# Residual state kept in HBM during the up projection, its memory used for early weight blocks of the down projection

## The chip, the cores and the metric

The kernel runs on one core of one Trainium2 chip, in one launch. The metric is device microseconds of the run. In the profile PE is TensorE's matmuls and PEld its weight loads, DVE is VectorE, ACT ScalarE, POOL GpSimd and SP SyncE, which issues most of the transfers.

## The reference

One layer of a decoder for 256 tokens of width 2048, all in float32. Shortened:

```python
def layer(x, p, mix_norm_g, w_in, ..., w_out, ffn_norm_g, w_up, conv_w, conv_b, w_down, ple_norm_g, w_ple_gate, w_ple_proj):
    h = rms_norm(x, mix_norm_g)
    z = h @ w_in                                   # one projection for both groups of mixers
    a = mlstm(z)                                   # 4 matrix-memory heads, chunkwise
    b = forgetting_attention(z)                    # 8 causal heads with log-forget bias
    x = x + concat([a, b]) @ w_out
    u = rms_norm(x, ffn_norm_g) @ w_up             # (256, 2 * 5632)
    u = gelu(causal_dwconv(u[:, :5632], conv_w, conv_b)) * u[:, 5632:]
    x = x + u @ w_down
    return x + sigmoid(rms_norm(x, ple_norm_g) @ w_ple_gate) * (p @ w_ple_proj)
```

The inner width is 5632, which is 44 blocks of 128 ("K tiles") of the down projection.

## The kernel before

**Products in float32.** Each weight block of 128 x 1024 values (512 KB) is loaded from HBM into a raw buffer by SP, cast by ScalarE to a high part `hi` (L969, L282 in the first stages), and VectorE makes the low part `lo = raw - hi` (L970, L284). PE then does three matmuls for each product, hi x hi, hi x lo and lo x hi, into a PSUM bank of 128 x 512. The step that needs one block is a *unit*. A unit of the up projection or of a plain pair has 12 matmuls. There are three raw buffers, and four buffers for parts; from the down projection on, two more buffers for parts exist (`w2`, made free by an earlier tile), two more raw buffers (`w2raw`), and later further rooms for raw blocks: `pT`, the two halves of `EZ` and part of `Y` (`ring`). `free_raws` says which rooms a block may use, and the loop in `run_units` loads a block as soon as a room is free and splits units up to six ahead of the unit that PE works on.

**The residual state.** `xs` holds x, 256 tokens by 2048 columns, as two tiles of 128 tokens: 2 MB of SBUF. The output projection's column groups add their results to `xs` (`resid`, L785), 512 columns at a time, square-sum them and send them to be transposed (squares on VectorE, then moves into `x2z` issued by POOL, then columns scaled into `x2T`). During the up projection nothing reads or writes `xs`. It is read again by `sums_done` (L1117 to L1122) and `add_rest` (L1130) at the end of each half of the down projection.

**Up projection.** Eleven groups of 16 units each. After a group, ScalarE scales the result into `EZ` (L869), VectorE transposes 32 x 32 squares (L193), POOL issues moves back into `EZ` (L199), and `up_act` does the convolution (L886 on ScalarE, eight L889 on VectorE), the GELU (L895), the gate product (L896) and the split into high and low parts (L138 for `uC`). For the last group these jobs are hung behind units of the down projection, at the positions (5, 6, 6, 7, 8, LAST_UP) with LAST_UP = 9.

**Down projection.** It has two halves of 1024 columns, and each goes through 22 pairs of K tiles. A plain pair is two units with four products each. The nine pairs in `SEVEN` use seven block products in place of eight (a Strassen-like scheme) and are four units with 1, 2, 2 and 2 products: for them VectorE also makes four differences of the raw blocks (L1065, L1066, L1075, L1076), and sums of the left operand are computed in the up projection, stored in HBM by POOL (L855) and loaded again by SP. The products that more than one result needs (P1, P5, P6, P7) gather in banks of their own (`dnP`), and `sums_done` adds them to `xs` behind the last of the sevens. `FIRST` gives the order of the pairs in the first half; the second half goes in the order 0 to 21. In the first half the last four pairs on the list are 19, 18, 20 and 21.

**What sets the order.** The program is written in units, but the build lets a scheduler order the instructions of each engine within the dependencies, so an instruction can stand at another place in its engine's queue than in the code. Each engine then runs its queue in order. SP's queue of loads is also in order: a load that waits holds the loads behind it.

Of the kernel before, what the change touches and what calls it, by code (L numbers as in the profile page):

```python
# [9 lines left out]
F32 = mybir.dt.float32  # L10
# [5 lines left out]
P = 128  # L16
S = 256
NT = S // P
D = 2048
# [5 lines left out]
KF = FF // P  # L25
# [7 lines left out]
BLK = 1024  # L33
# [1 line left out]
PARTS2 = 2  # L35

SEVEN = (2, 4, 6, 8, 10, 12, 14, 16, 18)
FIRST = (0, 1, 3, 5, 2, 7, 4, 6, 9, 8, 11, 10, 13, 12, 15, 14, 17, 16, 19, 18, 20, 21)
AHEAD_DMA, AHEAD_SPLIT = 3, 3
PAD = 16  # L40


LO_SHIFT = 16
FRONT = 12
LAST_UP = 9


@with_exitstack
def layer_kernel(
# [6 lines left out]
    nc = tc.nc  # L56
    act, dve, pe, pool = nc.scalar, nc.vector, nc.tensor, nc.gpsimd
# [7 lines left out]
    mp = mixers.enter_context(tc.tile_pool(name="mix", bufs=1))  # L65
    kp = ctx.enter_context(tc.tile_pool(name="kept", bufs=1, space=bass.MemoryType.DRAM))
    ps = ctx.enter_context(tc.tile_pool(name="ps", bufs=4, space=bass.MemoryType.PSUM))

    def bank(tag, name):
        return ps.tile([P, 512], F32, tag=tag, name=name)  # L70
# [11 lines left out]
    xs = bp.tile([P, NT, D], F32, name="xs")  # L82
# [61 lines left out]
    def transpose_x(dst, k0, g, tag="aux"):  # L144

        for k in (k0, k0 + 1):
            bk = bank(tag, f"xT{k}")
            for t in range(NT):
                pe.transpose(bk[:, t * P : (t + 1) * P], xs[:, t, k * P : (k + 1) * P], ident)
            split_T(dst[:, k, :], bk[:, 0:256], scale=g[:, k : k + 1])  # L150

    def sumsq(ssq, c, n):
        for t in range(NT):
            junk = sm.tile([P, 512], F32, tag="junk", name="junk")[:, :n]
            act.activation(junk, xs[:, t, c * n : (c + 1) * n], AF.Square, accum_out=ssq[:, t, c : c + 1])
# [29 lines left out]
    def squares(name):  # L185

        return mp.tile([P, NT, 4, 128], F32, tag="sq", name=name)

    def square(y, t, k, src):

        n = src.shape[1] // P
        o = y[:, t, :, 32 * k : 32 * (k + n)].rearrange("p b (k j) -> p k b j", j=32)
        dve.transpose(o, src)  # L193
# [7 lines left out]
    def gather(y, name):  # L201
        c = mp.tile([P, NT * 4, 128], F32, tag="col", name=name)
        move(y, c)
        return c, done[0]
# [8 lines left out]
    def columns(yz, dst, k0, gain):  # L213

        c, start = yz
        while not since(7, start):
            yield
        for k in range(4):
            column(c, k, dst()[:, k0 + k], gain[:, k0 + k : k0 + k + 1])
            yield  # L220
# [159 lines left out]
    with mixers:  # L380
# [399 lines left out]
        def resid(c, ssq, dst, gain):  # L780
            st = {}

            def f(t, b):
                xc = xs[:, t, c * 512 : (c + 1) * 512]
                dve.tensor_add(xc, b, xc)  # L785
                if c < 3:
                    if t == 0:
                        st["y"] = squares("x2y")
                    square(st["y"], t, 0, xc)
                if t == NT - 1:  # L790
                    if c < 3:
                        side.append(columns(gather(st["y"], "x2z"), dst, c * 4, gain))
                    else:
                        for k0 in (c * 4, c * 4 + 2):
                            transpose_x(dst(), k0, gain)
                    sumsq(ssq, c, 512)
            return f

        kcat = all_k[4:] + all_k[:4]
# [17 lines left out]
    with tc.tile_pool(name="ffn", bufs=1) as fp:  # L817
        x2 = x2T["t"]
# [15 lines left out]
        ring = Y[:, 0:1536].rearrange("p (r c) -> p r c", r=3)  # L834
# [5 lines left out]


        sums = kp.tile([len(SEVEN), P, 1024], F32, name="sums")

        def left_sums(p_, u):

            (a11, a21), (a12, a22) = ((u[:, j, 0:P], u[:, j, P:S]) for j in range(2))
            f = sm.tile([P, 512], F32, tag="junk", name="Sf").rearrange("p (i c) -> p i c", i=4)
            dve.tensor_add(f[:, 0], a21, a22)
            dve.tensor_sub(f[:, 1], f[:, 0], a11)
            dve.tensor_sub(f[:, 2], a11, a21)  # L850
            dve.tensor_sub(f[:, 3], a12, f[:, 1])
            t = fp.tile([P, 4, 256], F32R, tag="pT", name="Sp")
            act.copy(t[:, :, 0:P], f)
            dve.tensor_sub(t[:, :, P:256], f, f32(t[:, :, 0:P]))
            pool.dma_start(out=sums[SEVEN.index(p_)], in_=f32(t).rearrange("p i c -> p (i c)"))  # L855
# [48 lines left out]
        late = {}  # L904
        made, now = [0], [0]
        room = {"raw": RAW}
        taken, used = deque(), {}

        def free_raws(j):

            def may(t):
                return (t not in ("pT", "ring") or j < late["gate"]) and (t not in ("e0", "e1", "ring") or now[0] > late["free"])

            return sorted((t for t in room if taken.count(t) < room[t] and may(t)), key=lambda t: used.get(t, -1))

        def new_raw(j, name):
            tag = free_raws(j)[0]
            taken.append(tag)
            used[tag] = len(used) and max(used.values()) + 1
            if tag == "ring":  # L920
                return ring[:, 0:2].rearrange("p a b -> p (a b)")
            if tag in ("e0", "e1"):
                return EZ[:, int(tag[1])]
            if tag == "raw":
                return wp.tile([P, BLK], F32, tag="raw", name=name, bufs=RAW)
            if tag == "late":
                if tag not in late:
                    late[tag] = apool.tile([P, 2, BLK], F32, tag="aTb", name="w2raw", bufs=2)
                    late["n"] = 0
                late["n"] += 1  # L930
                return late[tag][:, late["n"] % 2]
            return fp.tile([P, BLK], F32, tag=tag, name=name, bufs=room[tag])
# [42 lines left out]
        def run_units(us, first_late, gate):  # L975
            loaded = split = 0
            for i, u in enumerate(us):
                if i == first_late:
                    v = apool.tile([P, 6, BLK], F32R, tag="aTa", name="w2", bufs=2)
                    room.update(late=2, pT=1, e0=1, e1=1, ring=1)  # L980
                    late.update(gate=gate, free=i + LAST_UP + 1, hi=v[:, 0:2], lo=v[:, 2:4],
                                S=v[:, 4:6].rearrange("p b (i c) -> p b i c", c=256))
                more = i >= first_late
                now[0] = i
                while True:
                    if loaded < len(us) and sum(room[t] - taken.count(t) for t in free_raws(loaded)) >= len(us[loaded].srcs):
                        us[loaded].load(loaded)
                        loaded += 1
                    elif split < min(loaded, i + PARTS + PARTS2 * more):
                        us[split].split(split)  # L990
                        for _ in range(us[split].frees):
                            taken.popleft()
                        split += 1
                    else:
                        break
                u.fn(*u.parts)
# [108 lines left out]
        def sums_done(c0):  # L1105

            def f(b):
                both = xs[:, 1, c0 : c0 + 1024].rearrange("p (n c) -> p n c", n=2)
                x00, x01 = (xs[:, 0, c0 + n * 512 : c0 + (n + 1) * 512] for n in range(2))
                right = xs[:, :, c0 + 512 : c0 + 1024]  # L1110

                def twice(v):
                    return v.unsqueeze(1).broadcast_to([P, 2, 512])

                a = ring[:, 2]
                act.copy(a, b["P1"])
                dve.tensor_add(x00, b["P1"], x00)  # L1117
                dve.tensor_add(a, b["P6"], a)
                dve.tensor_add(right, twice(b["P5"]), right)
                dve.tensor_add(both, twice(b["P7"]), both)  # L1120
                dve.tensor_add(x01, x01, a)
                dve.tensor_add(both, both, twice(a))  # L1122
            return f
# [31 lines left out]
        pT = {}  # L1155
# [82 lines left out]
        def with_after(u, hook):  # L1238
            fn = u.fn
            u.fn = lambda hi, lo: (fn(hi, lo), hook())  # L1240
# [26 lines left out]
        us = []  # L1267
        for q in range(KF // 4):
            us += up_group(q)
        first_late = len(us)  # L1270
        us += down(0, "aux", "mm", sums_done(0), add_rest(0), {}, FIRST)
        us += down(1024, "mm", "aux", sums_done(1024), add_rest(1024),
                   {23: x3_squares(0), 27: x3_squares(1),
                    31: x3_columns(0, 1, 2, 3), 35: x3_columns(4, 5, 6, 7)}, range(KF // 2))
        for c0, n in ((0, 512), (512, 512), (1024, 512), (1536, 512)):
# [10 lines left out]
            at = len(g_) // 2  # L1286
            us += g_[:at] + p_ + g_[at:]
        for q in range(KF // 4):
            for i, job in enumerate(up_act(q)):
                at = (8, 9, 10, 11, 12, 13) if q < KF // 4 - 1 else (5, 6, 6, 7, 8, LAST_UP)  # L1290
                with_after(us[KD * (q + 1) + at[i]], job)
        run_units(us, first_late, gate_at)


# [28 lines left out]
```

## Time and profile before

| what | value |
|---|---|
| median of three runs | 1254.27 us (1253.22 to 1254.82) |
| profiled execution, its own time | 1255.1 us |
| its span and granted clock of TensorE | 1253.4 us, 0.998 |
| busy PE, DVE, ACT, POOL | 1243.8, 832.2, 684.9, 210.4 us |
| HBM read, written | 246.54 MB, 6.83 MB |
| down projection's loads of weights into `raw` | 512 KB each, median 6.0 us from issue to landing |
| output projection's loads of weights | 512 KB each, median 4.5 us |

Times of instructions are microseconds from the start of the span, in one profiled execution. The span is the profiled part of the execution's time, so sums made on the span are compared with 1255.1 us, which lies 0.8 us above the median of the runs. PE's matmuls are pipelined: one takes 0.39 us, and the next starts 0.23 us after it. In a row of a timeline the bracket at the end gives the idle time before the instruction and who released it.

### The profile page before, as it was taken

What the parts mean: (1) busy time and instruction counts of PE and PEld (TensorE: products, weight loads), DVE (VectorE), ACT (ScalarE), POOL (GpSimd) and SP (SyncE); (2) the same over time, 40 slices, a digit from 0 to 9 for tenths busy, and PEclk for the clock granted to TensorE, in tenths of its full rate; (3) what the DMA queues carried; (4) which work ended last, traced back from release to release, by engine and by line L of the source; (5) the groups of instructions that cost most, each with busy time, mean ns of one, the idle gap of its engine ahead of it and who ended that gap; (6) DMA issues with size and microseconds to landing.
All of it is one profiled execution on the core that took longest, in us unless ns stands there. A gap on an engine that the chain in (4) does not pass through costs nothing.

```text
span 1253.4 us, 16510 instructions
## 1 busy us (share of the span) xinstructions
PE 1243.8 (99%) x5887; PEld 1051.4 (84%) x5887; DVE 832.2 (66%) x1055; ACT 684.9 (55%) x964; POOL 210.4 (17%) x395
## 2 busy tenths in 40 slices
PE   9999999999999999999999999999999999999998
PEld 7899988888888888888888888888886888888887
DVE  6455568754565655665676576667669998899553
ACT  7655555545554544655565566556546555556542
POOL 2003034100214202112202220221120000050000
PEclk9999999999999999999999999999999999999999
DMA  8667766656667767778877877887897886787560
GB/s 257 177 191 198 216 201 200 191 163 171 201 185 219 218 187 211 211 221 243 235 221 217 247 232 221 224 249 211 243 270 252 291 299 201 258 259 234 172 224 34
DMA packets 133476, 271.27 MB, mean 216 GB/s; under 512 B 14007, under 2 KB 28977, under 8 KB 133393
## 3 DMA queue, kind: packets, MB, share of 16 engines
q1 hardware_dynamic: 119936, 246.51, 65.7%
q0 software_dynamic: 13072, 23.53, 6.6%
q8 instruction: 46, 0.75, 0.2%
q14 instruction: 37, 0.30, 0.1%
q10 hardware_dynamic: 385, 0.16, 0.0%
HBM read 246.54 MB, written 6.83 MB: 202 GB/s over the span
## 4 chain that ended last, share of the span: by engine, by line
PE 95%; DMA 2%; DVE 1%; ACT 1%; issue 1%; POOL 0%; SPq 0%; DVEq 0%; ACTq 0%
PE up L1257 13%; PE up L1258 13%; PE up L1256 13%; PE tg L314 10%; PE tg L313 10%; PE tg L315 10%; PE wg L345 5%; PE wg L346 2%; DMA EZ<-Y 1%; PE dnP L1018 1%; PE dnP L1019 1%; PE dnP L1017 1%; PE dn(1, 0)_8870 L1018 1%; PE dn(0, 1)_8866 L1018 1%; PE dn(0, 1)_8866 L1017 1%; PE dn(0, 0)_8862 L1018 1%
## 5 line engine op out<-in xcount | busy, mean ns | idle before, releaser
L970 DVE TENSOR_TENSOR lo<-raw,hi 128x1024 fp32r<-128x1024 f32 (+1 forms) x219 | 264.4, 1209 | 181.9 <-ACT hi L969 181.6
L969 ACT CAST hi<-raw 128x1024 fp32r<-128x1024 f32 (+1 forms) x219 | 227.3, 1041 | 236.7 <-DMA raw<-in_w_up_dram 126.9
L284 DVE TENSOR_TENSOR lo<-raw,hi 128x1024 fp32r<-128x1024 f32 (+2 forms) x161 | 178.4, 1112 | 149.2 <-ACT hi L282 142.7
L282 ACT CAST hi<-raw 128x1024 fp32r<-128x1024 f32 (+2 forms) x161 | 153.7, 960 | 149.4 <-PE tg L315 81.6
L1258 PE MATMUL up<-hi,x2T 128*128 128x512 f32 x528 | 205.5, 389 | 0.0
L1257 PE MATMUL up<-lo,x2T 128*128 128x512 f32 x528 | 205.4, 389 | 0.0
L1256 PE MATMUL up<-hi,x2T 128*128 128x512 f32 x528 | 204.8, 389 | 0.0
L199 POOL DMA_DIRECT2D EZ<-Y x176 | 93.1, 536 | 175.8 <-DVE Y L193 143.1
L1256 PEld LDWEIGHTS up<-hi,x2T 128*128 128x128 f32 x528 | 99.1, 188 | 20.6
L1258 PEld LDWEIGHTS up<-hi,x2T 128*128 128x128 f32 x528 | 99.1, 188 | 20.5
L1257 PEld LDWEIGHTS up<-lo,x2T 128*128 128x128 f32 x528 | 99.1, 188 | 20.5
L314 PE MATMUL tg<-lo,hT 128*128 128x512 f32 (+1 forms) x288 | 102.9, 357 | 0.0
L313 PE MATMUL tg<-hi,hT 128*128 128x512 f32 (+1 forms) x288 | 101.8, 358 | 0.0
L315 PE MATMUL tg<-hi,hT 128*128 128x512 f32 (+1 forms) x288 | 101.7, 354 | 0.0
L1257 PE MATMUL up<-lo,x2Tb 128*128 128x512 f32 x176 | 68.5, 389 | 0.0
L1258 PE MATMUL up<-hi,x2Tb 128*128 128x512 f32 x176 | 68.5, 389 | 0.0
L345 PE MATMUL wg<-hT,hi 128*128 128x512 f32 x192 | 67.6, 399 | 0.0
L1256 PE MATMUL up<-hi,x2Tb 128*128 128x512 f32 x176 | 65.2, 389 | 0.0
L314 PEld LDWEIGHTS tg<-lo,hT 128*128 128x128 f32 x288 | 54.1, 188 | 5.5
L315 PEld LDWEIGHTS tg<-hi,hT 128*128 128x128 f32 x288 | 54.1, 188 | 5.5
L313 PEld LDWEIGHTS tg<-hi,hT 128*128 128x128 f32 x288 | 53.7, 188 | 5.4
L346 PE MATMUL wg<-hT,lo 128*128 128x256 f32 x192 | 52.1, 284 | 0.0
(762 smaller groups left out, 2428.1 us busy)
## 6 DMA issues: line engine op xcount, KB each, us to landing
raw<-in_w_up_dram SPq DMA_DIRECT2D x176, 512.0 KB, 4.9
raw<-in_w_in_dram SPq DMA_DIRECT2D x79, 512.0 KB, 4.1
raw<-in_w_down_dram SPq DMA_DIRECT2D x43, 512.0 KB, 6.0
raw<-in_w_in_dram SPq DMA_DIRECT2D x48, 344.0 KB, 3.6
raw<-in_w_out_dram SPq DMA_DIRECT2D x32, 512.0 KB, 4.5
EZ<-Y POOLq DMA_DIRECT2D x176, 64.0 KB, 5.6
w2raw<-in_w_down_dram SPq DMA_DIRECT2D x19, 512.0 KB, 5.7
w<-sums SPq DMA_DIRECT2D x18, 512.0 KB, 4.4
```

Of the source, the lines that this page charges most:

```text
L199: pool.dma_start(out=c[32 * b : 32 * b + 32, a::4], in_=y[32 * a : 32 * a + 32, :, b])
L282: act.copy(hi, raw[:, :w])
L284: dve.tensor_sub(lo, raw[:, :w], f32(hi))
L313: pe.matmul(o, ah, hi[:, i, :], start=first, stop=False)
L314: pe.matmul(o, ah, lo[:, i, :], start=False, stop=False)
L315: pe.matmul(o, al, hi[:, i, :], start=False, stop=last)
L345: pe.matmul(o, h[:, i, cols], a, start=first, stop=False)
L969: act.copy(hi, raw)
L970: dve.tensor_sub(lo, raw, f32(hi))
L1256: pe.matmul(o, ah, hi[:, n], start=k == 0, stop=False)
L1257: pe.matmul(o, ah, lo[:, n], start=False, stop=False)
L1258: pe.matmul(o, al, hi[:, n], start=False, stop=k == KD - 1)
```

## The change

The output projection's `resid` stores each 512 columns of `xs`, once they are summed, to an HBM tile `kept_x` (four stores of 512 KB, issued by POOL behind the square sums). From the first unit of the down projection on, the rooms for raw blocks include four more, `x0` to `x3`, quarters of `xs`, allowed for its units 0 to 19. `load_xs` fetches the whole state back, 2 MB in one transfer on SP's queue, hung behind unit 20. `FIRST` begins with six plain pairs in place of four, and the sevens follow in another arrangement; the jobs of the last group's `up_act` are hung one to two units later.

In the built order the four blocks that use `xs` are units 8 to 11 of the down projection, each room being used once. The scheduler puts their loads far ahead in SP's queue: two behind the load of the output projection's unit 150 and ahead of that of 151, and two in the first units of the up projection, ahead of the load of its unit 7. They wait for the stores of their columns. The transfer back stands in SP's queue ahead of the load of the down projection's unit 22. In POOL's queue each store stands ahead of the moves into `x2z` of its columns. PE, DVE and ACT have the same number of instructions as before.

```diff
--- before.py
+++ after.py
@@ -35,14 +35,15 @@
 PARTS2 = 2
 
 SEVEN = (2, 4, 6, 8, 10, 12, 14, 16, 18)
-FIRST = (0, 1, 3, 5, 2, 7, 4, 6, 9, 8, 11, 10, 13, 12, 15, 14, 17, 16, 19, 18, 20, 21)
+FIRST = (0, 1, 3, 5, 7, 9, 2, 4, 11, 6, 13, 8, 10, 15, 12, 17, 14, 16, 19, 18, 20, 21)
 AHEAD_DMA, AHEAD_SPLIT = 3, 3
 PAD = 16
 
 
 LO_SHIFT = 16
 FRONT = 12
-LAST_UP = 9
+X_LATE = 20
+LAST_UP = 11
 
 
 @with_exitstack
@@ -65,6 +66,8 @@
     mp = mixers.enter_context(tc.tile_pool(name="mix", bufs=1))
     kp = ctx.enter_context(tc.tile_pool(name="kept", bufs=1, space=bass.MemoryType.DRAM))
     ps = ctx.enter_context(tc.tile_pool(name="ps", bufs=4, space=bass.MemoryType.PSUM))
+
+    kept_x = kp.tile([P, NT, D], F32, name="kept_x")
 
     def bank(tag, name):
         return ps.tile([P, 512], F32, tag=tag, name=name)
@@ -794,6 +797,7 @@
                         for k0 in (c * 4, c * 4 + 2):
                             transpose_x(dst(), k0, gain)
                     sumsq(ssq, c, 512)
+                    pool.dma_start(out=kept_x[:, :, c * 512 : (c + 1) * 512], in_=xs[:, :, c * 512 : (c + 1) * 512])
             return f
 
         kcat = all_k[4:] + all_k[:4]
@@ -840,6 +844,9 @@
 
 
         sums = kp.tile([len(SEVEN), P, 1024], F32, name="sums")
+
+        def load_xs():
+            nc.sync.dma_start(out=xs, in_=kept_x)
 
         def left_sums(p_, u):
 
@@ -909,6 +916,8 @@
         def free_raws(j):
 
             def may(t):
+                if t[0] == "x":
+                    return j < late["first"] + X_LATE
                 return (t not in ("pT", "ring") or j < late["gate"]) and (t not in ("e0", "e1", "ring") or now[0] > late["free"])
 
             return sorted((t for t in room if taken.count(t) < room[t] and may(t)), key=lambda t: used.get(t, -1))
@@ -919,6 +928,9 @@
             used[tag] = len(used) and max(used.values()) + 1
             if tag == "ring":
                 return ring[:, 0:2].rearrange("p a b -> p (a b)")
+            if tag[0] == "x":
+                i = int(tag[1])
+                return xs[:, i // 2, i % 2 * BLK : (i % 2 + 1) * BLK]
             if tag in ("e0", "e1"):
                 return EZ[:, int(tag[1])]
             if tag == "raw":
@@ -977,8 +989,8 @@
             for i, u in enumerate(us):
                 if i == first_late:
                     v = apool.tile([P, 6, BLK], F32R, tag="aTa", name="w2", bufs=2)
-                    room.update(late=2, pT=1, e0=1, e1=1, ring=1)
-                    late.update(gate=gate, free=i + LAST_UP + 1, hi=v[:, 0:2], lo=v[:, 2:4],
+                    room.update(late=2, pT=1, e0=1, e1=1, ring=1, x0=1, x1=1, x2=1, x3=1)
+                    late.update(gate=gate, first=first_late, free=i + LAST_UP + 1, hi=v[:, 0:2], lo=v[:, 2:4],
                                 S=v[:, 4:6].rearrange("p b (i c) -> p b i c", c=256))
                 more = i >= first_late
                 now[0] = i
@@ -1287,8 +1299,9 @@
             us += g_[:at] + p_ + g_[at:]
         for q in range(KF // 4):
             for i, job in enumerate(up_act(q)):
-                at = (8, 9, 10, 11, 12, 13) if q < KF // 4 - 1 else (5, 6, 6, 7, 8, LAST_UP)
+                at = (8, 9, 10, 11, 12, 13) if q < KF // 4 - 1 else (6, 7, 8, 9, 10, LAST_UP)
                 with_after(us[KD * (q + 1) + at[i]], job)
+        with_after(us[first_late + X_LATE], load_xs)
         run_units(us, first_late, gate_at)
```

## The prediction

> **What bounds the kernel now.** I read the page's busy times and chain first, then the waits of TensorE (PE) around the place where the change acts, then PE's timeline there, then windows of that stage.
>
> ```profile
> span 1253.4 us, 16510 instructions
> PE 1243.8 (99%) x5887; PEld 1051.4 (84%) x5887; DVE 832.2 (66%) x1055; ACT 684.9 (55%) x964; POOL 210.4 (17%) x395
> ...
> PE 95%; DMA 2%; DVE 1%; ACT 1%; issue 1%; POOL 0%; SPq 0%; DVEq 0%; ACTq 0%
> ```
>
> PE is busy for 99% of the span and carries 95% of the chain, and the change leaves PE's instructions the same in number. So it can win only where PE idles or runs at a lower clock. The waits of PE from 900 to 1000 us, and its timeline, columns start, duration, line, operands, and the idle time before with its releaser:
>
> ```profile
> PE dn(1, 0)_8007 L1017 <- ACT hi L969: 1.3, 1, 1.3
> PE dnP L1018 <- DVE w L970: 1.2, 1, 1.2
> ```
>
> ```profile
> 914.55 0.39 PE L1017 MATMUL dn(0, 0)_7999<-hi,uA 128*128 128x512 f32 x1
> ...
> 950.34 0.50 PE L1018 MATMUL dnP<-w 128*128 128x512 f32 x1 [1.15 <-DVE w L970]
> ...
> 952.81 0.50 PE L1017 MATMUL dn(1, 0)_8007<-hi,uA 128*128 128x512 f32 x1 [1.28 <-ACT hi L969]
> ...
> 954.28 0.50 PE L1017 MATMUL dn(0, 0)_7999<-hi,uAb 128*128 128x512 f32 x1 [0.45 <-ACT hi L969]
> ...
> 954.86 0.63 PE L1018 MATMUL dn(1, 0)_8007<-lo,uA 128*128 128x512 f32 x1
> ...
> 957.85 0.58 PE L1018 MATMUL dn(0, 0)_7999<-lo,uAb 128*128 128x512 f32 x1
> 958.26 0.39 PE L1019 MATMUL dn(0, 0)_7999<-hi,uAb 128*128 128x512 f32 x1
> ```
>
> Three gaps, 1.15 + 1.28 + 0.45 = 2.9 us, stand in one place. Behind them come matmuls of 0.63 us in place of 0.39. The windows give the clock (columns: PE, PEld, DVE, ACT, POOL busy, PEclk, DMA share, GB/s):
>
> ```profile
> 914.60:941.00 26.40, 26.40 (x118) 21.81 (x117) 17.87 (x18) 13.68 (x16) 8.48 (x16) 1.00 0.91 257
> 941.00:955.00 14.00, 11.11 (x47) 8.21 (x46) 12.72 (x20) 9.79 (x13) 0.00 (x0) 0.99 0.73 245
> 955.00:960.00 5.00, 5.00 (x17) 3.93 (x16) 4.96 (x6) 1.66 (x3) 0.00 (x0) 0.68 1.01 315
> 960.00:1000.00 40.00, 39.89 (x175) 32.25 (x174) 38.88 (x44) 24.42 (x28) 0.00 (x0) 1.00 0.84 278
> 1000.00:1028.30 28.30, 28.30 (x127) 23.43 (x126) 26.41 (x30) 16.63 (x18) 0.00 (x0) 1.00 0.84 285
> ```
>
> From 954.86 to 958.26, 3.4 us, PE ran at half speed and lost 1.7 us; PE's other idle in 960 to 1000 is 0.11. So the first half of the down projection gives away 2.9 + 0.1 + 1.7 = **4.7 us**, 0.38%, and this is all that the change can win. In the windows VectorE (DVE) is the near-bound: idle 8.5 us before 941, but only 1.3 + 0.0 + 1.1 + 1.9 = 4.3 us from there to 1028, while PE itself lost 4.7.
>
> **The change, part by part.**
>
> *The order of the pairs.* DVE's durations (count, busy us, mean ns):
>
> ```profile
> L970 DVE TENSOR_TENSOR lo<-raw,hi 128x1024 fp32r<-128x1024 f32 x21 | 25.5, 1220 | 10.4 <-ACT hi L969 10.4
> L970 DVE TENSOR_TENSOR lo<-raw,hi 128x512 fp32r<-128x512 f32 x5 | 3.4, 686 | 1.4 <-ACT hi L969 1.4
> L889 DVE SCALAR_TENSOR_TENSOR Y<-Y,cT 128x255 f32<-128x255 f32 (+1 forms) x16 | 6.9, 476 | 0.4 <-ACT Y L886 0.4
> L1065 DVE TENSOR_TENSOR raw<-raw 128x512 f32<-128x512 f32 x4 | 2.8, 688 | 0.1
> L896 DVE TENSOR_TENSOR Y<-Y,EZ 128x1024 f32<-128x1024 f32 x2 | 2.4, 1224 | 0.6 <-ACT Y L895 0.6
> L138 DVE TENSOR_TENSOR uC<-Y,uC 128x1024 fp32r<-128x1024 f32 x2 | 2.4, 1216 | 0.0
> ```
>
> A plain pair costs DVE two splits, 2.4 us, and PE 24 matmuls; 118 matmuls in 26.40 us are 0.224 each, with the window's cut edges 0.225, so 5.4 us. A seven-product pair costs DVE 3 x 1.22 + 0.69 + 4 x 0.69 = 7.1 us, 6.9 when the pieces run back to back, and PE 21 matmuls, 4.7 us. So each plain pair gives DVE 3.0 us of lead and each seven takes 2.2. The last group's activation (8 x 0.43 + 1.22 + 1.22 = 5.9 us, 0.43 being 6.9/16) comes on top and starts here:
>
> ```profile
> 941.02 1.06 ACT L881 COPY Y<-EZ 128x1024 f32<-128x1024 f32 x1 [0.69 <-DMA EZ<-Y]
> ```
>
> Splits run at most six units ahead of PE. In the kernel before, pair 2 is units 8 to 11, a plain pair 12 and 13, and pair 4 units 14 to 17. By 941 PE is in unit 9, so DVE can be done with unit 13 at best; to come before PE needs unit 17 (914.55 + 8 x 2.7 + 4.7 + 5.4 + 15 matmuls, 3.4, = 949.7) are 6.9 + 5.9 = 12.8 us, until 953.8. That is 4 us late by this sum where 2.9 were measured, since PE has high-part products to do meanwhile. In the changed order pair 4 is units 16 to 19. By 941 DVE reaches unit 14; unit 15 (2.6), pair 4 (6.9) and the activation (5.9) last until 956.4, and PE needs unit 19 at 914.55 + 32.4 + 4.7 + 3.4 = 955.1: 1.3 us late, 0.9 by the same shrink. The built order puts two splits of later units in front, 1.14 + 0.60, so up to 3.0. I take **1.2** (bounds 0 and 3.0): the old place loses most of its idle time.
>
> What is late next is the rest of the half. The old order has one place where two sevens stand side by side (4 and 6 are neighbours); the new one has three: 2 and 4, 8 and 10, 14 and 16. Each takes 4.4 us of lead, and the lead is short: after the first, 3.0 - 2.2 + 3.0 = 3.8 us are won back, then 4.4 taken. That is 0.6 short at the second and, after 15, 12 and 17 in the same way, 0.6 at the third. The built order of the instructions makes both worse. At pair 8, ScalarE's cast for a unit of pair 10 waits for a buffer that PE frees when it is done with the second unit of pair 8, and the cast of pair 8's fourth unit is queued behind it; PE has only the third unit, 6 matmuls or 1.35 us, to cover two casts:
>
> ```profile
> L969 ACT CAST w<-raw 128x1024 fp32r<-128x1024 f32 x12 | 12.5, 1052 | 10.0 <-PE dn(1, 1)_8011 L1019 4.1 <-PE dn(1, 0)_8007 L1019 2.1 <-PE dnP L1019 1.7
> ```
>
> 2 x 1.05 - 1.35 = 0.7, and the next cast a little later again: **1.4** (bounds 0 and 3). At the end of the half the additions of the P banks are queued on DVE (1.21 for a 128x1024 one, 0.68 for a 512) among the splits of pair 18 and of pairs 20 and 21; two 1.21 additions in front of splits that PE waits for are **2.4** (bounds 0 and 4). Sum of new idle 1.2 + 1.4 + 2.4 = 5.0, against 3.0 that go. In the kernel before the last place costs nothing, which is what speaks most against this term.
>
> *The clock.* PE fell to half speed behind gaps of 1.15 and 1.28 within 3.6 us; a single gap did not do it:
>
> ```profile
> 7.62 0.66 PE L149 MATMUL xT<-ident,xs 128*128 128x128 f32 x4 [1.29 <-DMA xs<-in_x_dram]
> 8.35 0.39 PE L314 MATMUL tg<-lo,hT 128*128 128x512 f32 x1
> ```
>
> The new idle is in pieces of about 0.5 to 1.3 over some 60 us, so I take no drop, and the 1.7 us come back; a drop costs 1.7 for each place. The Trainium skill (TensorE: Matmul & The Clock Gate, "Part 1: The HAM clock gate") says that PE goes to half rate after an idle window of about 3.4 us. The trace differs: no gap was over 1.28 us and the rate was halved all the same, for 3.4 us. By the page no drop could occur in either kernel; by the row one more may, 1.7 us on my sum.
>
> *The store of xs and four early loads.* Each column block's store is issued by GpSimd (POOL), and the four loads into xs stand early in SP's queue, two of them ahead of the load of w_out's unit 151, behind the landing of the second store. The nearest store and the rows around it:
>
> ```profile
> L855 POOL DMA_DIRECT2D sums<-Sp x9: 563/563/587, 561.9 to 909.8; - x9
> ...
> DMA to landing us min/median/max: 4.6/5.8/7.0
> ```
>
> ```profile
> 391.11 1.28 DVE L785 TENSOR_TENSOR xs<-tg,xs 128x512 f32<-128x512 f32 x2
> 396.31 0.37 SPq L267 DMA_DIRECT2D raw<-in_w_out_dram  x1
> 400.94 1.05 ACT L282 CAST hi<-raw 128x1024 fp32r<-128x1024 f32 x1 [2.86 <-DMA raw<-in_w_out_dram]
> 410.70 1.05 ACT L282 CAST hi<-raw 128x1024 fp32r<-128x1024 f32 x1 [1.72 <-PE tg L315]
> ```
>
> xs is summed at 392.4, the store lands 397.0 to 399.4, and unit 151's load, issued at 396.31 before and landed 4.6 later, now goes at 397.8 to 400.2 behind 1 MB more (3.5 us at 300 GB/s, about the 315 of the window above). It lands at 406 to 408 and is cast 1.1 later, 407 to 409. PE starts on it at 407.9 (it frees unit 151's buffer for the cast at 410.70, 2.7 later). So 0 to 2 us; I take **0.5**. The copies of x2z are queued on POOL behind the store's issue and start 0.6 later, and their columns are read by PE only in the next stage, so 0. The Trainium skill (DMA: Bandwidth & Descriptors, "Anatomy of one DMA — SWDGE (gpsimd) path") gives 2.0 us plus bytes/436e3, an estimate of 3.2 for 512 KB; the row says 4.6 to 7.0, and the measurement decides. By the page this term would be 0. The other two loads go before w_up's unit 7, with more slack; 0.
>
> *Load of xs back.* 2 MB, 7 us at 285 GB/s, on SP's queue before the loads of unit 22 on; four units' loads, as many bytes, are gone from the stretch before 941 (257 GB/s, share 0.91). First use of xs is about 80 us later. Cost 0; without that cover the loads behind it come 7 us later (a rival).
>
> **Sum.** -4.7 + 5.0 + 0.5 = +0.8 us. The profiled run took 1255.1 us, 0.8 above the median of 1254.27, so on the median 1255.1. About 0.2%, 2.5 us, is what a measurement of this kernel can tell from no change.
>
> **The rivals.** *The stall simply goes* (26%): the queue inversions at pairs 8 and 18 are absorbed as in the kernel before, where the end of the half had 28.30 of 28.30 us busy. Then 1.2 or less stays: -4.7 + 1.2 = -3.5, 1250.8, and 1249.6 at best. For it: 4.3 us of idle DVE after 941. Against: three double sevens.
> *Slower by the clock* (20%): if two of the new places lose over 2.4 us within some 3.6, as at 949 to 953, PE runs 3.4 us at half speed behind each: 2 x 1.7 on top of +0.8, 1258.5. It decides at the end of the half first. For it: the 2.4 us there; against: shorter pieces.
> *Slower by w_out* (12%): stores at 7.0 us or later starve units 151 and 152 by 2 us and their gap costs a half-speed window: +0.8 + 1.5 + 1.7, 1258.3. Against: the cast of 400.94 ended 5.9 us before PE's need.
> *It does nothing of what it says*: the four early blocks hide loads that were hidden anyway, DVE waits only for the six-unit rule; the forecast already holds that.
>
> **Numbers.** The forecast has 42%, 1252.5 to 1257; the others as above. Faster by over 0.2%: 0.26; within: 0.42; slower: 0.32. The range reaches from 1250.0 to 1259.5.
>
> **What would show it.** Right: no gap at 949 to 954 in its old form, PE idle at the neighbouring sevens and at the end of the half, 4 to 6 us in all; PEclk 1.0 or one dip; DVE busy over 95% from 947 on; under 1 us at unit 151. Wrong: PE idle under 2 us in that half, or over 2 us in w_out, or PEclk halved twice.

## The result and the profile after

The changed kernel takes 1256.22 us (median of 20 runs) against 1254.5 (20 runs): ratio 1.0015, 95% interval 1.0008 to 1.0022. It is a little slower, by 1.9 us on the ratio. One of the 20 runs took 4245 us, far slower than all others, and the ratio leaves it out.

The profiled execution of the kernel after took 1257.1 us, 0.9 above its median. Of its page, the lines that answer to those shown of before:

```profile
span 1255.4 us, 16510 instructions
PE 1245.0 (99%) x5887; PEld 1049.4 (84%) x5887; DVE 831.7 (66%) x1055; ACT 684.3 (55%) x964; POOL 214.0 (17%) x399
...
PE 89%; DMA 5%; DVE 3%; ACT 2%; issue 1%; POOL 0%; SPq 0%; DVEq 0%; ACTq 0%
```

The busy times hardly differ. The chain does: PE carries 89% in place of 95%, and transfers 5% in place of 2%, so stretches before which the chain could run back along PE alone now have a wait in them. To see where, three moments of PE are enough: its first matmul of the output projection, of the down projection, and of the gate that follows. The timeline of before (start, duration, line, operands), then of after:

```profile
346.72 0.39 PE L313 MATMUL tg<-hi,catT 128*128 128x512 f32 x1
...
1146.07 0.39 PE L313 MATMUL tg<-w,x3T 128*128 128x512 f32 x1
```

```profile
346.17 0.39 PE L316 MATMUL tg<-hi,catT 128*128 128x512 f32 x1
...
915.47 0.39 PE L1029 MATMUL dn(0, 0)_8008<-hi,uA 128*128 128x512 f32 x1
...
1148.14 0.39 PE L316 MATMUL tg<-w,x3T 128*128 128x512 f32 x1
```

With the 914.55 of before, the output and up projections took 567.83 us before and 569.30 after, **+1.47**; the down projection took 231.52 before and 232.67 after, **+1.15**. Up to 346 us the kernel after is 0.55 ahead, which is a shorter wait for x at the start (0.54 us in place of 1.29) and none of the change's doing. Together +2.07 at the last matmul, and 2.0 in the span.

The waits of PE in the down projection of after (us in total, times, longest), and the same windows as before:

```profile
PE dnP L1030 <- DVE lo L982: 1.0, 1, 1.0
PE dn(1, 0)_8016 L1029 <- ACT w L981: 0.9, 1, 0.9
PE dn(1, 0)_8016 L1029 <- ACT hi L981: 0.8, 2, 0.6
PE dn(0, 0)_8008 L1029 <- ACT hi L981: 0.4, 2, 0.2
PE dn(1, 0)_8016 L1030 <- DVE lo L982: 0.4, 1, 0.4
PE dn(0, 0)_8008 L1030 <- DVE w L982: 0.2, 1, 0.2
PE dn(0, 0)_8865 L1029 <- ACT hi L981: 0.2, 1, 0.2
```

```profile
914.60:941.00 26.40, 26.40 (x118) 21.88 (x117) 18.63 (x18) 14.80 (x17) 8.51 (x16) 1.00 0.95 284
941.00:955.00 14.00, 14.00 (x64) 11.54 (x63) 10.16 (x17) 8.08 (x12) 0.00 (x0) 1.00 0.66 224
955.00:960.00 5.00, 3.58 (x14) 1.76 (x12) 5.00 (x7) 5.00 (x6) 0.00 (x0) 1.00 0.70 236
960.00:1000.00 40.00, 38.81 (x167) 30.73 (x167) 37.54 (x43) 20.26 (x23) 0.00 (x0) 1.00 0.79 275
1000.00:1028.30 28.30, 26.92 (x116) 21.11 (x115) 26.61 (x30) 16.38 (x18) 0.00 (x0) 1.00 0.79 263
```

The old stall is gone: 14.00 of 14.00 us busy from 941 to 955. In its place PE idles in three clusters: four gaps of 1.8 us in all at 955 to 962, two of 0.8 at 985 to 987, and three of 1.4 at 1022 to 1026. No half clock shows in this execution (PEclk 1.00). DVE is idle 3.8 us from 941 to 955, while it waits for casts, and is then at its limit.

### The profile page after: what moved, and what is told of

Same layout as the page of the kernel before. It is cut to its first block, busy times and chain, and to the rows that moved or that the text cites. A ratio compares the mean times of both kernels' runs of the same rounds, so it can differ in the third digit from the quotient of the medians.

```text
span 1255.4 us, 16510 instructions
## 1 busy us (share of the span) xinstructions
PE 1245.0 (99%) x5887; PEld 1049.4 (84%) x5887; DVE 831.7 (66%) x1055; ACT 684.3 (55%) x964; POOL 214.0 (17%) x399
## 4 chain that ended last, share of the span: by engine, by line
PE 89%; DMA 5%; DVE 3%; ACT 2%; issue 1%; POOL 0%; SPq 0%; DVEq 0%; ACTq 0%
PE up L1269 12%; PE up L1270 12%; PE up L1268 12%; PE tg L317 9%; PE tg L316 9%; PE tg L318 9%; PE wg L348 5%; PE wg L349 2%; DMA raw<-in_w_out_dram 2%; DMA EZ<-Y 1%; PE dnP L1031 1%; PE dnP L1030 1%; PE dnP L1029 1%; DMA raw<-in_w_up_dram 1%; DVE lo L982 1%
## 5 line engine op out<-in xcount | busy, mean ns | idle before, releaser
L982 DVE TENSOR_TENSOR lo<-raw,hi 128x1024 fp32r<-128x1024 f32 (+1 forms) x228 | 274.6, 1207 | 180.0 <-ACT hi L981 179.1
L981 ACT CAST hi<-raw 128x1024 fp32r<-128x1024 f32 (+1 forms) x228 | 236.1, 1039 | 249.3 <-DMA raw<-in_w_up_dram 144.2
```

The source lines that it names most:

```text
L981: act.copy(hi, raw)
L982: dve.tensor_sub(lo, raw, f32(hi))
```

## The experiments

In the table the ratio is to the kernel before in the same rounds (medians 1254.0 to 1254.7 us). The two stages are first matmul to first matmul in each run's profile, as above; "half clock" says whether PE ran at half speed in that execution's down projection.

| run | median us | ratio to before (95%) | output + up | down | half clock |
|---|---|---|---|---|---|
| before | 1254.5 | 1 | 567.83 | 231.52 | 3.4 us |
| after | 1256.2 | 1.0015 (1.0008 to 1.0022) | 569.30 | 232.67 | none |
| e1 order alone | 1258.1 | 1.0031 (1.0020 to 1.0042) | 567.83 | 234.02 | 3.4 us |
| e2 rooms alone | 1254.5 | 1.0002 (0.9993 to 1.0010) | 567.92 | 229.58 | none |
| e3 load later | 1255.7 | 1.0012 (1.0003 to 1.0022) | 569.61 | 234.80 | 3.4 us |
| e4 store later | 1256.8 | 1.0023 (1.0013 to 1.0033) | 570.67 | 232.28 | none |
| e5 other order, no rooms | 1250.0 | 0.9969 (0.9957 to 0.9981) | 567.83 | 226.88 | none |
| e6 early loads held | 1255.4 | 1.0009 (1.0000 to 1.0019) | 567.83 | 233.94 | 3.4 us |
| e7 e6, order of e5 | 1248.8 | 0.9961 (0.9948 to 0.9973) | 567.84 | 225.31 | none |
| e8 double seven moved | 1257.7 | 1.0036 (1.0022 to 1.0049) | 569.65 | 234.64 | none |
| e9 e6, load back held | 1254.2 | 1.0002 (0.9993 to 1.0010) | 567.84 | 230.38 | none |
| e10 e6, other end | 1251.5 | 0.9975 (0.9966 to 0.9984) | 567.83 | 227.98 | none |
| e11 e9, sevens apart | 1250.4 | 0.9966 (0.9955 to 0.9977) | 567.83 | 225.75 | none |
| e12 e9, order of e5 | 1250.4 | 0.9973 (0.9962 to 0.9984) | 567.84 | 225.95 | none |

**e1, the order alone.** On the kernel before: `FIRST`, `LAST_UP` and the places of `up_act` as in the change.

```diff
-FIRST = (0, 1, 3, 5, 2, 7, 4, 6, 9, 8, 11, 10, 13, 12, 15, 14, 17, 16, 19, 18, 20, 21)
+FIRST = (0, 1, 3, 5, 7, 9, 2, 4, 11, 6, 13, 8, 10, 15, 12, 17, 14, 16, 19, 18, 20, 21)
-LAST_UP = 9
+LAST_UP = 11
```

> The new order of the pairs and the later activation alone: no store of xs, no early blocks, no load back. Theory (the new idle comes from the order; the store and the early loads cost 1.5 us on the way to the up projection and help the first sevens): PE's down projection starts as in the kernel before (914.6, against 915.5 with the change); idle at the end of the half (1.2 to 1.5 us) and at pairs 8 and 10 (about 0.8) stays; without the early blocks the rooms are short where 2 and 4 stand side by side, so the idle at 947 to 962 grows from 1.8 to 4 us or more: about 1257 us or more. Rival (the early blocks do nothing for PE): same idle as with the change, no loss in the output projection, 1256.2 - 1.5 = 1254.7 us.

No loss on the way to the down projection, and the same three clusters. The time came, 1258.1 us, but not for the reason that I gave: the first cluster is not larger than with early blocks (1.3 us of idle against 1.8), against my theory; the 3.4 us at half clock stand at the end of the half. Its windows of 955 to 960 and 1022 to 1030:

```profile
955.00:960.00 5.00, 3.90 (x14) 2.39 (x15) 5.00 (x6) 3.31 (x4) 0.00 (x0) 1.00 1.00 357
...
1022.00:1030.00 8.00, 7.17 (x22) 5.15 (x23) 6.79 (x6) 1.28 (x2) 0.00 (x0) 0.79 0.86 274
```

**e2, the rooms alone.** The changed kernel with the old `FIRST`, `LAST_UP` and places.

> The store of xs, the early blocks and the load back, with the old order of the pairs and the old places of the activation. Theory (the old stall is made by the old order, by VectorE's work at 949 to 954): gaps of about 2.9 us stay there, with or without the half clock, and the loss of 1.5 us on the way to the up projection is there: 1254.5 + 1.5 = 1256.0 us. Rival (the old stall came from late blocks, and early blocks remove it): 1254.5 - 4.7 + 1.5 = 1251.3 us.

The old stall stays, a little later and in another shape, as the theory says (2.6 us of idle at 952 to 961); early blocks do not remove it. The time is 1.5 us lower than I gave: in this execution the loss before the down projection was only 0.09 us, so that term lies at the edge of its slack. PE's waits:

```profile
PE dnP L1029 <- ACT hi L981: 1.2, 1, 1.2
PE dn(1, 0)_8016 L1029 <- ACT hi L981: 0.8, 1, 0.8
PE dn(0, 0)_8008 L1029 <- ACT hi L981: 0.7, 2, 0.5
```

**e3 and e4, the load back later, the stores later.**

```diff
-        with_after(us[first_late + X_LATE], load_xs)
+        with_after(us[first_late + X_LATE + 16], load_xs)
```

> The changed kernel with the load of xs hung 16 units later (behind unit 36 of the down projection in place of 20). Theory (the 2 MB that go out at 934.3 hold up the last of the moves into EZ, which landed 3.2 us later than before, and with them the last activation): ScalarE's copy out of EZ goes back from 944.2 to about 942, the first cluster of idle (955 to 962, 1.8 us) falls under 1, time about 1255.2 us. Rival (the moves are late because of the loads of weights, and the first cluster comes from the two sevens side by side): copy at 944, cluster 1.5 to 2, 1256.2 us.

```diff
-                    pool.dma_start(out=kept_x[:, :, c * 512 : (c + 1) * 512], in_=xs[:, :, c * 512 : (c + 1) * 512])
...
+        for c, j in enumerate((32, 48, 64, 80)):
+            with_after(us[j], lambda c=c: pool.dma_start(out=kept_x[:, :, c * 512 : (c + 1) * 512], in_=xs[:, :, c * 512 : (c + 1) * 512]))
```

> The changed kernel with the four stores of xs hung behind units 32, 48, 64 and 80 of the up projection, so that the four early loads wait until then. Theory (the early loads ahead of w_out's unit 151 and of w_up's unit 7 cost 0.62 + 0.85 us): the gaps at 407.8, 438.3 and 455.8 are gone, PE's down projection starts about 1.4 us earlier than in the changed kernel, time 1256.2 - 1.4 = 1254.8 us. Rival (it is not their place but the traffic that costs; the same loads cost as much inside the up projection): gaps appear in the up projection, 1256.2 us.

Neither answers its question: nothing that comes late holds these transfers, so the scheduler put them where they were. In e3 the load back went out at 935.26, in e4 the fourth store at 442.34. They are further executions of the changed kernel, and show that its loss before the down projection varies: 1.78 and 2.84 us beside 1.47.

**e5, another order, and nothing else changed.**

```diff
-FIRST = (0, 1, 3, 5, 2, 7, 4, 6, 9, 8, 11, 10, 13, 12, 15, 14, 17, 16, 19, 18, 20, 21)
+FIRST = (0, 1, 3, 5, 2, 7, 9, 4, 11, 6, 13, 8, 15, 10, 17, 12, 19, 14, 16, 20, 18, 21)
```

> The kernel before with only the order of the pairs changed: 0, 1, 3, 5, 2, 7, 9, 4, 11, 6, 13, 8, 15, 10, 17, 12, 19, 14, 16, 20, 18, 21. Two plain pairs stand between 2 and 4, where the last activation falls, and after that a plain pair stands behind each seven but one (14 and 16). No store of xs, no early blocks. Theory (each double seven takes 4.4 us of VectorE's lead, and the old stall is pair 4's splits and the activation at the same time): the idle at 949 to 954 goes to under 0.7 us and no new idle over 0.7 us appears at the end of the half; with the half clock gone too about 1254.4 - 4 = 1250.4 us. Rival (the stall comes from late blocks or from the activation alone, whatever pair is beside it): 2 to 3 us of idle stay at 947 to 960, 1254 us.

As the theory said: 0.7 us of idle in three small gaps at 955 to 958, none later, and 0.31% faster than before.

**e6, the early loads held by a real dependency.**

```diff
                     if k == KD - 1:
+                        if 2 <= q < 6:
+                            j = q - 2
+                            dve.tensor_add(held[:, j : j + 1], xs[:, j // 2, j % 2 * BLK : j % 2 * BLK + 1], EZ[:, 0, 0:1])
                         up_turn()
```

> The changed kernel with the early loads held back by a real dependency: behind the last unit of the up projection's groups 2, 3, 4 and 5 VectorE adds one column of a quarter of xs to one of that group's results, into a scratch tile, and the load into that quarter has to wait for it. The result of these four small additions is not used. Theory (the two loads ahead of unit 151 and the two ahead of w_up's unit 7 cost 1.5 us, in the repeat e4 2.8): the gaps at 407 to 410, 438 and 455 are gone, PE's down projection starts within 0.2 us of the kernel before, no gap in the up projection; 1256.2 - 1.5 = 1254.7 us. Rival (the same bytes cost as much at any place): gaps in the up projection, 1256.2 us.

The stage is back at 567.83 us, as in the other eight profiles with held or no early loads (567.83 or 567.84); the five profiles with them at the place of the change (e2, after, e3, e8, e4) lost 0.09, 1.47, 1.78, 1.82 and 2.84 us. The cost is in their place, not in the traffic. The times alone do not show it: the intervals of e6 and of the change overlap, e6's runs spread from 1253.1 to 1257.8 us, and its profile is the slowest of them. How the cost comes about, in after's timelines of POOL, SP, ScalarE and PE:

```profile
392.13 0.68 POOL L800 DMA_DIRECT2D kept_x<-xs  x1 [10.29 <-DVE xs L788]
397.12 0.82 SPq L967 DMA_DIRECT2D xs<-in_w_down_dram  x2
398.03 14.00 SPq L270 DMA_DIRECT2D raw<-in_w_out_dram  x6
405.74 1.05 ACT L285 CAST hi<-raw 128x1024 fp32r<-128x1024 f32 x1 [8.20 <-DMA raw<-in_w_out_dram]
408.10 0.50 PE L317 MATMUL tg<-lo,catT 128*128 128x512 f32 x1 [0.32 <-DVE lo L287]
438.47 0.50 PE L1269 MATMUL up<-lo,x2T 128*128 128x512 f32 x1 [0.15 <-DVE lo L982]
```

The store is issued at 392.13, the two early loads at 397.12, unit 151's load behind them at 398.03 in place of 396.31, and its cast starts at 405.74 in place of 400.94. The low part is late for PE.

**e7, e6 with the order of e5.**

> e6 with the order of the pairs of e5. Theory (the early blocks do nothing that PE sees once the order is right): the time of e5, 1250.4 us, within 1 us. Rival (early blocks let VectorE and ScalarE start earlier and help the first seven): faster than e5 by 1 us or more. Third possibility (the load of xs back delays the moves into EZ and the activation): slower than e5 by 0.5 to 1.5 us with idle at 950 to 960.

No wait of PE in the half at all. In the profiles it is 1.6 us faster than e5 in the down projection, which speaks for the rival: early blocks remove the small gaps left. It is not shown: the two ratios' intervals overlap, and e7 also has the change's later places for the jobs of `up_act`, which e5 has not.

**e8, the double seven moved.** The changed kernel with 15 between 8 and 10. With 12, 14 and 16 in a row the sums of pair 16 are fetched into the buffer that pair 12's last product still needs, so that product uses other sums and the output is wrong; no work is left out.

> The changed kernel with pair 15 put between 8 and 10, which leaves 12, 14 and 16 in a row later: 0, 1, 3, 5, 7, 9, 2, 4, 11, 6, 13, 8, 15, 10, 17, 12, 14, 16, 19, 18, 20, 21. Theory (idle comes where sevens stand side by side): the idle at 985 (0.8 us) goes, 0.5 to 1.5 us appear between 990 and 1012, the first cluster and the end of the half stay; 1256.2 to 1257.5 us. Rival (the idle at 985 belongs to the time or to pair 8, not to the neighbours): it stays at 985.

Its two gaps behind the first cluster:

```profile
986.02 0.50 PE L1030 MATMUL dn(1, 0)_8016<-lo,uB 128*128 128x512 f32 x1 [1.33 <-DVE lo L982]
1008.62 0.50 PE L1029 MATMUL dnP<-hi,w 128*128 128x512 f32 x1 [1.18 <-DMA w<-sums]
```

The theory's second part came (a new gap where three sevens stand, though it is the sums that are late), its first did not: idle stays at 985, now behind DVE. So this run could not tell neighbours from the lack of lead.

**e9, the load back held too.** On e6:

```diff
                 act.copy(by_run(a_), runs(Z[:, :, 0:128]))
+                if q == KF // 4 - 1:
+                    dve.tensor_add(held[:, 0:2], xs[:, 0, 0:2], a_[:, 0, 0:2])
```

> e6 with a further real dependency: the load of xs back waits until ScalarE has copied the last group out of EZ, so that its 2 MB cannot share the transfers with the last moves into EZ (a small addition on VectorE that reads xs and the copy; its result is not used). Theory (those 2 MB hold up the moves, the copy starts at 944 to 945 in place of 941, and VectorE's activation falls on the two sevens): copy at 939 to 942, first cluster of idle (1.7 to 1.9 us in four gaps) under 0.7, the other two places stay: 1255.4 - 2 = 1253.4 us. Rival (the first cluster comes from 2 and 4 side by side; without the load back, in e1, it cost as much): copy earlier, cluster as before, 1255.4 us or more, since the load now lands later.

The theory held in the profile: the first cluster is gone, two gaps of 0.1 remain. By the ratios it is 0.9 us faster than e6, not 2, and the two intervals overlap. After, then e9: SP's load back, ScalarE's copy that needs the moves, and what the 16 moves took to land:

```profile
934.34 0.33 SPq L849 DMA_DIRECT2D xs<-kept_x  x1
944.23 1.05 ACT L888 COPY Y<-EZ 128x1024 f32<-128x1024 f32 x1 [2.98 <-DMA EZ<-Y]
...
DMA to landing us min/median/max: 6.4/6.9/9.3
```

```profile
939.27 1.05 ACT L889 COPY Y<-EZ 128x1024 f32<-128x1024 f32 x1 [1.73 <-DMA EZ<-Y]
940.54 0.33 SPq L850 DMA_DIRECT2D xs<-kept_x  x1
...
DMA to landing us min/median/max: 5.9/6.5/7.6
```

The copy starts 24.7 us behind the first matmul of the down projection, against 28.8 in after and 26.5 in the kernel before. In after a cast is queued behind the waiting copy, and VectorE waits 3.75 us for it at 942.5; in e9 all of the activation but its last split is through by 948.9, when VectorE begins pair 4's differences.

The other profiles agree. In the five where the load back went out before the last move was issued (after, e3, e4, e6, e8), the last move took 8.5 to 9.6 us to land and the copy started 28.4 to 30.0 us behind the first matmul of the down projection; in the five where it went out behind the copy (e2, e7, e9, e11, e12) these are 5.9 to 6.9 and 24.2 to 25.1, and in the three that have no load back 6.2 to 6.7 and 25.3 to 26.5.

e9 and e1 have the same order of the pairs and the same places of `up_act`; e9 adds the rooms, with both of their costs held off. Its ratio is 1.0002 against 1.0031, intervals apart, and its first cluster 0.1 us of idle against 1.3. So with this order the freed memory does help.

**e10, another end of the order.** On e6: 14, 19, 16, 20, 18, 21 at the end.

> e6 with only the end of the order changed: ... 8, 10, 15, 12, 17, 14, 19, 16, 20, 18, 21 in place of 14, 16, 19, 18, 20, 21. Theory (14 and 16 side by side take the lead that the additions at the end of the half then need): the three gaps at 1023 to 1026 (1.4 us, and now and then a stretch at half clock) go, the gaps at 955 to 962 and at 985 stay: 1255.4 - 2.4 = 1253.0 us. Rival (the additions behind the last seven cost that anyway, whatever pairs stand in front): gaps of 1 us or more stay at the end of the half, 1255 us.

The end of the half has no gap left, and 0.8 us at 982 stay. Against what I expected, the first cluster was small here too, 0.2 us, and the time 1.5 us lower than given: its copy started at 939.77 although the load back went out at 933.49. POOL had issued the last of its moves 1.2 us ahead of the load there, while in after the last one, at 934.7, came 0.4 behind it. So that collision depends on timing. What the end costs in after is read on ScalarE:

```profile
1017.38 0.59 ACT L1128 COPY Y<-dnP 128x512 f32<-128x512 f32 x1 [4.23 <-PE dnP L1031]
...
1022.61 1.04 ACT L981 CAST w<-raw 128x1024 fp32r<-128x1024 f32 x1
...
```

```profile
1023.70 0.50 PE L1029 MATMUL dn(1, 0)_8016<-w,uC 128*128 128x512 f32 x1 [0.93 <-ACT w L981]
```

`sums_done` starts with a copy of bank P1, and in the built order it stands ahead of seven casts. ScalarE waits 4.23 us for PE's last product into P1, then casts without a pause, and PE catches up at the sixth. In e10 the copy's wait is none, as in the kernel before. No run moves the copy alone, so this cause is read from the rows, not shown by an edit; that 14 and 16 side by side are not enough for it, e5 and e11 show, where they stand so and the end has no gap.

**e11, six plain pairs first and the sevens after 2 and 4 apart.** On e9: 0, 1, 3, 5, 7, 9, 2, 4, 11, 6, 13, 8, 15, 10, 17, 12, 19, 14, 16, 20, 18, 21.

> e9 (early loads held, load back held behind the copy out of EZ) with the order of e8 up to pair 12 and the end of e10: 0, 1, 3, 5, 7, 9, 2, 4, 11, 6, 13, 8, 15, 10, 17, 12, 19, 14, 16, 20, 18, 21. So the change's six plain pairs and its 2 and 4 side by side stay; 8 and 10 are parted, and 14 and 16 are followed by 20. In e8 the first cluster had eaten VectorE's lead just ahead of pair 8; here it has not. Theory (idle at 981 to 987 comes from 8 and 10 side by side once the lead is whole): no gap over 0.3 us in the whole half, about 1254.5 - 5 = 1249.5 us. Rival (as e8 suggests, the place at pair 8 to 10 idles whatever the neighbours): 0.8 to 1.3 us at 980 to 987, 1251 us.

No gap in the half. So, as the theory says, the idle at 981 to 987 belongs to 8 and 10 side by side when the lead is whole (e9); where the first cluster has eaten the lead, parting them is not enough (e8). Six plain pairs first, and 2 and 4 side by side behind them, do no harm by themselves once the load back is held, 8 and 10 are parted and the end is changed; the time is that of e5, which has neither. Windows:

```profile
941.00:955.00 14.00, 14.00 (x64) 11.59 (x63) 14.00 (x21) 10.00 (x12) 0.00 (x0) 1.00 0.97 337
...
960.00:1000.00 40.00, 40.00 (x179) 33.10 (x177) 37.81 (x44) 22.47 (x24) 0.00 (x0) 1.00 0.83 276
1000.00:1028.30 28.30, 28.30 (x126) 23.46 (x125) 25.11 (x28) 17.07 (x19) 0.00 (x0) 1.00 0.77 256
```

**e12, e7 with the load back held.**

> e7 with the load back held behind the copy out of EZ as in e9. In e7 the load back went out after the copy by itself. Theory (nothing is left to win in this half): the time of e7, 1248.8 us, within 0.8 us, no gap. Rival (the held load back delays the loads behind it on SP's queue and they become late): gaps at 950 to 975, slower than e7 by 1 us or more.

One gap of 0.16 us; the stage is within 0.7 us of e7's. The median is 1.6 us above e7's, outside what I gave, but with runs from 1248.65 to 1253.85 and overlapping intervals. e5, e7, e11 and e12 are not told apart by their times; all four beat both kernels.

## Why the prediction was right

The forecast was 1255.1, +0.8 us on the profiled sum; the runs give +1.9 on the ratio and +2.07 in the traces. The mechanism, the stall moves and does not go, is what happened, at the three places that were named. Of the signs, PE's idle came out at 4.0 us (4 to 6 given) and DVE was busy 94.9% of 947 to 1028 (over 95% given). By its steps:

- **What there was to win.** I took 4.7 us, idle plus half clock. The runs without gaps show more: before 231.52 us, e11 225.75, so 5.8. The step that failed is to count a gap at its idle time. In the row of 952.81 the idle is 1.28, but from the matmul before (951.14) to the one after (953.15) pass 2.01 us where two starts at 0.23 would take 0.46: 1.55 lost. Each gap costs about 0.27 on top, as PE fills again; this holds within 0.02 for all nine gaps of after's half.
- **The first cluster.** Predicted 1.2, measured 1.8 idle. Its size came out for a partly wrong reason. I costed the load back at 0 and looked for its harm in the loads behind it; e9 shows that it holds up the last moves into `EZ`, and with them the activation. In e1, with no load back and no early blocks, the cluster is there all the same, and in e9, with the blocks and without the collision, it is gone. So the blocks help and the load back harms in the same place, and that the size came out within 0.6 us is partly luck.
- **The second.** Predicted 1.4, measured 0.8. The queue was the right one, ScalarE's, but a pair later than I wrote: the cast for pair 12's second unit waits for a buffer that pair 10's second unit frees, and pair 10's last cast stands behind it. e9 and e11 show that the neighbours make it when the lead is whole. After's ScalarE, and PE's matmul that waits for the second of these casts:

```profile
983.68 1.05 ACT L981 CAST w<-raw 128x1024 fp32r<-128x1024 f32 x1 [1.28 <-PE dn(0, 1)_8012 L1031]
984.63 1.99 ACT L981 CAST hi<-raw 128x1024 fp32r<-128x1024 f32 x2
```

```profile
985.73 0.50 PE L1029 MATMUL dn(1, 0)_8016<-hi,uB 128*128 128x512 f32 x1 [0.57 <-ACT hi L981]
```

- **The end of the half.** Predicted 2.4, measured 1.4 of idle in three gaps, about 2.2 with the filling. I put it on VectorE's additions, and that step failed; by the rows it is ScalarE's copy of P1, which heads the same `sums_done`.
- **The clock.** I took no drop, with 1.7 us for one. Some executions have it and some do not: after and e4 none, e1 and e3 at the end of the half, e6 at the first cluster. In e1 and e3 it came behind gaps of 0.92, 0.22 and 0.23 us, less than the 1.15 and 1.28 from which I took what a drop needs. The kernel before varies in the same way: 1.7 of its 4.7 us are in the execution that I read and not in every one. Of its 30 runs beside the first experiments, 11 had a mean clock of 1.000, with a median span of 1252.0; 3.41 us at half speed alone make it 0.999, so these had none. The other 19 had lower ones, with 1253.2; some of these may have no such stretch but the one behind the last matmul (before has one there too, from 1251.8). So +1.15 in the half sets an execution with the half clock against one without; without those 1.7 it is +2.85.
- **The early loads.** Predicted 0.5 at w_out's unit 151 (bounds 0 to 2) and 0 at w_up's unit 7; measured 0.6 and 0.85, and 0.09 to 2.8 in all over five executions. The second store, for which the first two loads wait, landed in 4.8 us, inside the row that I used (4.6 to 7.0), and all four in 4.1 to 6.0:

```profile
DMA to landing us min/median/max: 4.1/4.8/6.0
```

The estimate of 3.2 us from the fit in the Trainium skill (DMA: Bandwidth & Descriptors, "Anatomy of one DMA — SWDGE (gpsimd) path") was short for these stores, and the term that it would have set to 0 was real. I had called w_up's part covered by "more slack"; that was not so in four of the five profiles.

The sum of the new idle in the half, 5.0 predicted against 4.0 measured, hid that filling adds 2.4 to nine gaps; the old stall was undercounted in the same way, so the difference for the half, +0.3 predicted and +1.15 measured, came out less wrong than its terms. That these errors cancel is luck, and so is the 0.55 us that after gained at its start; the three places where PE idles are not.

## What to carry to other kernels

When PE is fed by engines whose queues run in order, the order of the work decides whether a lead is spent in one place: spread the pieces that cost the feeders more than PE, and look in the built order for an instruction that waits on PE ahead of casts that PE needs. A transfer that is "free" by its bytes still has a place: ask what stands behind it on its queue and which small moves it shares the engines with. A later place in the program holds nothing back when no dependency does; if a transfer must wait, give it something to wait for.

## What the runs showed of the hardware

A gap in a stream of 128x512 matmuls costs about 0.27 us more than its idle time: the matmul ahead of it runs out its 0.39 us with no other started 0.23 behind it, and the first matmul behind it takes 0.50 us in place of 0.39 and the next starts 0.34 later in place of 0.23. In four profiles (before, e1, e3, e6) PE's clock was halved in the down projection, each time for 3.41 us, behind clusters whose longest single gap was 0.92 to 1.28 us; after, e2, e4 and e8 have clusters too, with longest gaps of 0.93 to 1.33 us, and no halving. The Trainium skill (TensorE: Matmul & The Clock Gate, "Part 1: The HAM clock gate") has that length as a window that runs freely; its rule that an idle window of that length is needed does not agree with these gaps. The same 2 MB load took 12.8 us to land when it met the moves in after, and 8.0 when it went out behind them in e9; over all profiles 11.6 to 13.3 against 7.8 to 8.0.
